# Moving every large SBUF tile from byte offset 64 to offset 0 within 128

## The chip, the cores and the metric

The kernel runs on one core of a Trainium2 chip. The metric is device time in microseconds, the median of several executions. A profile of one execution, with every instruction and every DMA packet, stands beside the times.

## The reference

One block of a streaming encoder, float32, 512 tokens of width 1024:

```python
proj = x @ w_in[layer]
q_a, k_a, v_a, q_i, k_i, w_i, q_s, k_s, v_s, g_a, g_b = jnp.split(proj, IN_OFFSETS, axis=-1)
w_i = w_i * IDX_HEADS ** -0.5
y_a = ...   # sparse attention, 8 heads of 64: an indexer (q_i, k_i, w_i) picks the 128 best keys of each query,
            # logits + relative bias, softmax, times v_a
y_s = ...   # stick-breaking attention, 8 heads of 64: exp(log_sigmoid(z) + sum of later log_sigmoid(-z)), times v_s
gate_a = jax.nn.sigmoid(g_a + b_gates[layer, 0])
gate_b = jax.nn.sigmoid(g_b + b_gates[layer, 1])
merged = gate_a * (y_a @ w_branch_dsa[layer]) + gate_b * (y_s @ w_branch_sb[layer])
x = layer_norm(DEEPNORM_ALPHA * x + merged @ w_out[layer], ln1_g[layer], ln1_b[layer])
u, g = jnp.split(x @ w_ffn_in[layer], 2, axis=-1)          # 2 x 2816 columns
h = jax.nn.gelu(causal_dwconv(u, conv_w[layer], conv_b[layer])) * g
x = layer_norm(DEEPNORM_ALPHA * x + h @ w_ffn_out[layer], ln2_g[layer], ln2_b[layer])
```

## The kernel before

**Precision.** Each operand of a product is split into a high part (rounded to the float32r type) and a low part (the rest), and each product is three matmuls: high x high, high x low, low x high. In the names, `h`/`hi` and `l`/`lo` are the two parts: `x1h` and `x1l` are the normed activations, `whi_u` and `wlo_u` a weight tile. Almost every matmul has a moving operand of 512 float32 columns (2 KB in a partition), with 384 in the first projection and 256 in some products.

**Weights.** The class `Stream` walks one list of pieces, mostly 128 x 1024 float32. For each, SP's queue loads a `raw` tile (L87), ACT makes the high part (L105), DVE or POOL the low part (L107). `raw` and the two rings have three buffers each, and loads and splits run three pieces ahead of use.

**Stages.** Indexer's projection `qi` (L249 to L251) and its keys `ki`; then attention heads, eight of each kind, with the remaining projections (`proj_t`, L285 to L287, and `proj_v`) and gates cut into groups of three matmuls and filled in between the heads' steps; transposes of the attention weights against `ident` (L420); branch projections, the output projection (L697 to L699) with the first norm; the FFN's two input products (`ffn_in`, L739 to L741), of which `u` goes through a causal convolution of width 3 (`activate`, L749 to L754), and the output product (`product`, L829 to L831), in which seven products of halves stand for eight; then the second norm. The order of the instructions on each engine is fixed when the program is built.

**Addresses.** SBUF is filled from both edges. Pools of tiles without a side are stacked upward from the left edge: first `cst` with the constants `ident` (512 bytes in each partition), `mhalf` (4), `bgt` (64), `cwt` (352) and `wi`, then the raw tiles, the rings and the stages' tiles. Pools with `side="right"` are stacked downward from the right edge; the first of them, `edge`, holds `rb` alone. An allocation begins at a multiple of 32 bytes, and large tiles take multiples of 128 bytes. Small ones are brought up to that by a helper:

```python
n = int(np.prod(shape[1:]))
t = pool.tile([shape[0], -(-n // 32) * 32], dt, **kw)[:, :n]
```

So all tiles of one side have the same offset within 128 bytes, and the first small tiles on that side set it. In the built program the tiles behind `cwt` and those behind `rb` all begin at 64 within 128 bytes; `ident`, against which transposes are made, begins at 0, `bgt` at 32 and `cwt` at 96.

`bgt` holds the gates' biases: 16 columns, read one at a time as ACT's bias (L546 and others). `rb` holds the relative bias table's high and low parts: 64 x 8, the weights of two matmuls (L270).

Of the kernel before, what the change touches and what calls it, by code (L numbers as in the profile page):

```python
# [11 lines left out]
F32 = mybir.dt.float32  # L12
F32R = mybir.dt.float32r
# [7 lines left out]
H = 8  # L21
# [109 lines left out]
def tile_block(ctx: ExitStack, tc: tile.TileContext, xT, xN, w_qi, w_ki, w_t, w_v, w_br, w_o, w_fi, w_fo,  # L131
# [10 lines left out]
    def padded(pool, shape, dt=F32, **kw):  # L142

        n = int(np.prod(shape[1:]))
        t = pool.tile([shape[0], -(-n // 32) * 32], dt, **kw)[:, :n]
        return t if len(shape) == 2 else t.rearrange("p (a b) -> p a b", a=shape[1])

    cst = ctx.enter_context(tc.tile_pool(name="cst", bufs=1))
    edge = ctx.enter_context(tc.tile_pool(name="edge", bufs=1, side="right"))
# [68 lines left out]
    nc.gpsimd.memset(mhalf, -0.5)  # L218
    nc.scalar.activation(mhalf, mhalf, AF.Sigmoid)
    nc.gpsimd.memset(mhalf, -0.5)  # L220
    bgt = cst.tile([128, 16], F32, name="bgt")
    cwt = cst.tile([128, FC, 4], F32, name="cwt")


# [31 lines left out]

    ohf = bp.tile([64, NREL], F32, tag="beta", bufs=2, name="ohf")
    oh = bp.tile([64, NREL], F32R, tag="beta", bufs=2, name="oh")
    rb = edge.tile([64, H], F32R, name="rb")
    rbf = padded(bp, [32, H], name="rbf")  # L260
    for r in (slice(0, 32), slice(32, 64)):
        nc.gpsimd.dma_start(ohf[r], onehot)
# [791 lines left out]
```

## Time and profile before

| | us |
|---|---|
| median of 3 executions | 762.42 |
| lowest, highest | 762.22, 762.43 |
| profiled execution | 762.05 |
| its span, first to last instruction | 760.2 |
| TensorE busy | 751.1 |
| VectorE, ScalarE, GpSimd busy | 547.1, 374.1, 119.3 |

The mean granted clock of TensorE over the span is 0.998 of full speed. PE stands for TensorE's matmuls, PEld for its weight loads, which run beside them, DVE for VectorE, ACT for ScalarE, POOL for GpSimd, SP for SyncE. A matmul's recorded duration includes its way through the array, so it is longer than the distance from its start to the next one's.

### The profile page before, as it was taken

The numbers are of one execution on the slowest core, as the hardware profiler recorded it, in microseconds if no ns is written. First come the engines' busy times: TensorE is split into PE (matmuls) and PEld (weight loads), VectorE is DVE, ScalarE is ACT, GpSimd is POOL, SyncE is SP. The second block draws the span as 40 slices with busy tenths as digits, with TensorE's granted clock in tenths as the row PEclk, the third lists the DMA queues.
The fourth block names the chain that finished last, engine by engine and source line by source line (L and its number), as shares of the span: only waits on it lengthen the run. The fifth ranks groups of instructions, "written<-read, shape, count | busy, mean of one in ns | idle before, by whom it ended". The sixth has DMA issues, their size and how long they took to land.

```text
span 760.2 us, 9908 instructions
## 1 busy us (share of the span) xinstructions
PE 751.1 (99%) x3597; PEld 630.3 (83%) x3597; DVE 547.1 (72%) x912; ACT 374.1 (49%) x601; POOL 119.3 (16%) x127
## 2 busy tenths in 40 slices
PE   9999999999999999999999999999999999999996
PEld 7788888888888888888889888888888888888885
DVE  6689587999675454458865778767877786777776
ACT  6554656555686857935311534433443443344320
POOL 3002555425834210000010000000000000000011
PEclk9999999999999999999999999999999999999999
DMA  8643423132333333126801554354434434445971
GB/s 258 225 155 100 123 83 111 57 111 84 111 98 97 102 106 99 55 78 203 328 1 42 166 181 147 117 180 170 135 138 164 169 129 147 168 153 157 340 291 56
DMA packets 38449, 107.09 MB, mean 141 GB/s; under 512 B 4536, under 2 KB 4936, under 8 KB 38400
## 3 DMA queue, kind: packets, MB, share of 16 engines
q1 hardware_dynamic: 34016, 95.73, 37.1%
q10 hardware_dynamic: 2576, 6.29, 3.2%
q0 software_dynamic: 1808, 4.44, 1.8%
q8 instruction: 28, 0.46, 0.2%
q14 instruction: 21, 0.17, 0.1%
HBM read 91.48 MB, written 12.87 MB: 137 GB/s over the span
## 4 chain that ended last, share of the span: by engine, by line
PE 92%; POOL 3%; issue 2%; DVE 2%; ACT 1%; DVEq 0%; POOLq 0%
PE u_ps L741 5%; PE u_ps L740 5%; PE g_ps L741 5%; PE u_ps L739 5%; PE g_ps L740 5%; PE g_ps L739 5%; PE m_ps L829 4%; PE m_ps L831 4%; PE m_ps L830 4%; PE av_ps L436 2%; PE ga_ps L285 2%; PE ga_ps L286 2%; PE ga_ps L287 2%; PE o_ps L698 2%; PE o_ps L699 2%
## 5 line engine op out<-in xcount | busy, mean ns | idle before, releaser
L739 PE MATMUL u_ps<-x1h,whi_u 128*128 128x512 f32 (+1 forms) x192 | 71.4, 372 | 0.0
L741 PE MATMUL u_ps<-x1h,wlo_u 128*128 128x512 f32 (+1 forms) x192 | 71.4, 372 | 0.0
L740 PE MATMUL u_ps<-x1l,whi_u 128*128 128x512 f32 (+1 forms) x192 | 71.3, 371 | 0.0
L739 PE MATMUL g_ps<-x1h,whi_g 128*128 128x512 f32 (+1 forms) x184 | 69.9, 380 | 0.0
L740 PE MATMUL g_ps<-x1l,whi_g 128*128 128x512 f32 (+1 forms) x184 | 69.9, 380 | 0.0
L741 PE MATMUL g_ps<-x1h,wlo_g 128*128 128x512 f32 (+1 forms) x184 | 69.9, 380 | 0.0
L748 POOL MEMSET u<- 128x2 f32 x22 | 2.1, 100 | 250.1 <-DVE c L753 250.1
L740 PEld LDWEIGHTS u_ps<-x1l,whi_u 128*128 128x128 f32 x192 | 36.2, 188 | 6.3
L739 PEld LDWEIGHTS u_ps<-x1h,whi_u 128*128 128x128 f32 x192 | 36.2, 188 | 6.2
L741 PEld LDWEIGHTS u_ps<-x1h,wlo_u 128*128 128x128 f32 x192 | 36.2, 188 | 6.2
L740 PEld LDWEIGHTS g_ps<-x1l,whi_g 128*128 128x128 f32 x184 | 34.6, 188 | 6.6
L739 PEld LDWEIGHTS g_ps<-x1h,whi_g 128*128 128x128 f32 x184 | 34.6, 188 | 6.5
L741 PEld LDWEIGHTS g_ps<-x1h,wlo_g 128*128 128x128 f32 x184 | 34.6, 188 | 6.5
L425 DVE TENSOR_TENSOR ptl<-tr_ps,pth 128x512 fp32r<-128x512 f32 (+1 forms) x48 | 27.4, 595 | 14.0 <-ACT pth L424 13.7
L107 DVE TENSOR_TENSOR wlo_u<-raw,whi_u 128x1024 fp32r<-128x1024 f32 x22 | 26.9, 1221 | 9.8 <-ACT whi_u L105 9.8
L105 ACT ACTIVATE whi_g<-raw 128x1024 fp32r<-128x1024 f32 x22 | 23.3, 1061 | 20.5 <-PE m_ps L831 13.6
L105 ACT ACTIVATE whi_pa<-raw 128x1024 fp32r<-128x1024 f32 x11 | 11.7, 1061 | 40.8 <-PE u_ps L740 32.3
L754 ACT ACTIVATE c<-c,cwt 128x512 f32<-128x512 f32 x22 | 15.8, 716 | 30.0 <-DVE c L753 30.0
L105 ACT ACTIVATE whi_u<-raw 128x1024 fp32r<-128x1024 f32 x22 | 23.3, 1060 | 13.9 <-PE u_ps L740 9.0
L107 DVE TENSOR_TENSOR wlo_g<-raw,whi_g 128x1024 fp32r<-128x1024 f32 x22 | 26.8, 1218 | 3.1 <-ACT whi_g L105 3.1
L488 POOL TENSOR_TENSOR bm<-win,score 128x256 f32<-128x256 f32 (+2 forms) x24 | 26.9, 1148 | 9.0 <-DVE mn L503 8.9
L758 DVE TENSOR_TENSOR hp<-g_ps,c 128x512 f32<-128x512 f32 x22 | 15.2, 691 | 17.3 <-PE g_ps L741 15.8
(559 smaller groups left out, 2205.9 us busy)
## 6 DMA issues: line engine op xcount, KB each, us to landing
raw<-in_w_fi_dram SPq DMA_DIRECT2D x44, 512.0 KB, 3.3
raw<-in_w_t_dram SPq DMA_DIRECT2D x32, 512.0 KB, 3.3
raw<-in_w_fo_dram SPq DMA_DIRECT2D x21, 512.0 KB, 3.5
rawb_p<-in_w_fo_dram SPq DMA_DIRECT2D x11, 512.0 KB, 3.7
d_z<-s_sum SPq DMA_DIRECT2D x10, 512.0 KB, 7.4
raw<-in_w_v_dram SPq DMA_DIRECT2D x8, 512.0 KB, 4.3
raw<-in_w_br_dram SPq DMA_DIRECT2D x8, 512.0 KB, 3.3
raw<-in_w_o_dram SPq DMA_DIRECT2D x8, 512.0 KB, 4.3
```

Source lines behind the costliest of these rows:

```text
L105: nc.scalar.activation(hi[:, :w], t[:, :w], AF.Copy)
L107: self.low = eng.tensor_sub(lo[:, :w], t[:, :w], r32(hi[:, :w])).ins
L285: nc.tensor.matmul(ps[:M], wh[:, c], xh[k], start=(k == 0), stop=False)
L425: lows = nc.vector.tensor_sub(tl[:, :width], ps[:, :width], r32(th[:, :width]))
L488: nc.gpsimd.tensor_add(bm[:, OFF[j]:OFF[j] + N], win[:, 512 - N:512], score[j])
L739: nc.tensor.matmul(ps[:, c], wh[:, kc], x1h[:, k, c], start=(k == 0), stop=False)
L740: nc.tensor.matmul(ps[:, c], wh[:, kc], x1l[:, k, c], start=False, stop=False)
L741: nc.tensor.matmul(ps[:, c], wl[:, kc], x1h[:, k, c], start=False, stop=(k == KC - 1))
L754: nc.scalar.activation(c, c, AF.Gelu_apprx_tanh, bias=cwt[:, f, 3:4])
L829: nc.tensor.matmul(o, xh_[:, r], wh[:, c], start=start, stop=False, skip_group_check=True)
L830: nc.tensor.matmul(o, xh_[:, r], wl[:, c], start=False, stop=False, skip_group_check=True)
L831: mm = nc.tensor.matmul(o, xl_[:, r], wh[:, c], start=False, stop=stop, skip_group_check=True)
```

## The change

Two small tiles are made 64 bytes longer, and the same slice of them as before is used: `bgt` at the left edge, from 64 to 128 bytes, and `rb` at the right edge, from 32 to 96 bytes. All that is stacked behind them moves by 64 bytes: upward on the left, downward on the right. In the built program these tiles then begin at 0 within 128 bytes; `cwt` begins at 32. No instruction is added, removed or moved.

```diff
@@ -218,7 +218,7 @@
     nc.gpsimd.memset(mhalf, -0.5)
     nc.scalar.activation(mhalf, mhalf, AF.Sigmoid)
     nc.gpsimd.memset(mhalf, -0.5)
-    bgt = cst.tile([128, 16], F32, name="bgt")
+    bgt = cst.tile([128, 32], F32, name="bgt")[:, :16]
     cwt = cst.tile([128, FC, 4], F32, name="cwt")
@@ -256,7 +256,7 @@
     ohf = bp.tile([64, NREL], F32, tag="beta", bufs=2, name="ohf")
     oh = bp.tile([64, NREL], F32R, tag="beta", bufs=2, name="oh")
-    rb = edge.tile([64, H], F32R, name="rb")
+    rb = edge.tile([64, 24], F32R, name="rb")[:, :H]
     rbf = padded(bp, [32, H], name="rbf")
```

## The prediction

> **What bounds the kernel now.** I read the page first, for who is busy and what the chain of waits consists of.
>
> ```profile
> span 760.2 us, 9908 instructions
> PE 751.1 (99%) x3597; PEld 630.3 (83%) x3597; DVE 547.1 (72%) x912; ACT 374.1 (49%) x601; POOL 119.3 (16%) x127
> ...
> PE 92%; POOL 3%; issue 2%; DVE 2%; ACT 1%; DVEq 0%; POOLq 0%
> ```
>
> TensorE is busy nearly from end to end and is 92% of the chain that ends last. Second, the table by stage, since a share over the whole span could hide a stage with another limit (columns: length, then busy time of PE, PEld, DVE, ACT, POOL, then clock, DMA share, GB/s).
>
> ```profile
> 0.00:21.00 21.00, 19.80 (x96) 16.75 (x97) 12.22 (x20) 12.70 (x21) 6.04 (x19) 1.00 0.86 264
> ...
> 50.00:160.00 110.00, 110.00 (x539) 92.81 (x538) 93.02 (x186) 64.40 (x116) 46.71 (x27) 1.00 0.31 94
> 160.00:208.00 48.00, 47.68 (x241) 40.02 (x240) 40.18 (x78) 27.95 (x55) 28.55 (x20) 1.00 0.34 104
> 208.00:330.00 122.00, 122.00 (x608) 102.83 (x607) 65.31 (x130) 91.12 (x167) 23.55 (x23) 1.00 0.29 92
> ...
> 414.00:690.00 276.00, 276.00 (x1261) 230.29 (x1259) 206.64 (x299) 119.05 (x165) 3.13 (x22) 1.00 0.45 152
> 690.00:744.00 54.00, 54.00 (x242) 44.78 (x241) 38.34 (x55) 16.86 (x19) 1.98 (x2) 1.00 0.76 267
> 744.00:760.30 16.30, 8.65 (x68) 8.25 (x66) 12.44 (x24) 0.51 (x1) 2.78 (x3) 0.91 0.18 65
> ```
>
> From 21 to 744 us PE never rests for long; only the last 16 us belong to DVE (12.44 us against PE's 8.65). Third, PE's own waits. There are two in the whole span:
>
> ```profile
> PE idle_ps L208 <- DVE idle L205: 1.2, 1, 1.2
> PE gb_ps L285 <- DVE va L337: 0.3, 1, 0.3
> ```
>
> So a DMA, ACT or DVE instruction that gets a few ns longer or shorter has almost nowhere to show. What counts is the time from one matmul's start to the next. Fourth, then, the timeline of PE, once for each width of moving operand: 512 columns in the FFN, 384 in the first projection (four merged in a row), 256 in the last product.
>
> ```profile
> 559.82 0.39 PE L740 MATMUL u_ps<-x1l,whi_u 128*128 128x512 f32 x1
> ...
> 561.86 0.39 PE L740 MATMUL u_ps<-x1l,whi_u 128*128 128x512 f32 x1
> ...
> 7.75 0.85 PE L249 MATMUL qi_ps<-xh,whi_qi 128*128 128x384 f32 x4
> 8.44 0.85 PE L250 MATMUL qi_ps<-xl,whi_qi 128*128 128x384 f32 x4
> ...
> 747.81 0.28 PE L829 MATMUL m_ps<-d_z,eh 128*128 128x256 f32 x1
> 747.93 0.28 PE L830 MATMUL m_ps<-d_z,eh 128*128 128x256 f32 x1
> ```
>
> Between the first two rows stand nine matmuls' starts: 2.04 / 9 = 227 ns for 512 columns. Then 0.69 / 4 = 173 ns for 384 and 120 ns for 256. From 256 to 512 columns the step is 107 ns, so 512 columns alone would take 2 x 107 = 214 ns, and each matmul carries about 13 ns that does not depend on its width (384: 173 - 160 = 13). This fixed 13 ns is the only thing in the profile through which a start address could move the time much. In the layout of the built program every moving operand of these matmuls starts at 64 within 128 bytes, so the trace has no row of the same matmul at 0.
>
> **The change part by part.** It adds, removes and reorders no instruction; on every engine the rows are the same. In the layout, 930 buffers counted from the left edge move up by 64 bytes and 97 counted from the right edge down by 64; all these stood at 64 and then stand at 0. cwt goes from 96 to 32; ident, mhalf and bgt stay. The extra columns of bgt and rb are never written or read: their DMA and their two DVE instructions have the same size, so 0 us.
>
> Weight loads. 3597, beside the matmuls (188 ns of 227). Here the trace has start offsets to compare: the eight slices of wlo_ki follow each other by 72 x 4 = 288 bytes, so they start at 64, 96, 0 and 32 within 128, twice over.
>
> ```profile
> L287 PEld LDWEIGHTS ki_ps<-xh,wlo_ki x8: 140/141/142, 23.2 to 28.1; 128*72 128x72 f32 x8
> ```
>
> Minimum to maximum 2 ns: the start offset is not seen. Cost 0; the cover is 227 - 188 = 39 ns a matmul, and losing it would need a load 39 ns longer.
>
> DVE and ACT. The convolution reads u at its start (64), and 4 and 8 bytes later, and ACT writes u 8 bytes later; the same shapes at 64 stand beside them.
>
> ```profile
> L752 DVE SCALAR_TENSOR_TENSOR c<-u,cwt,c x22: 743/745/754, 423.9 to 685.4; 128x512 f32<-128x512 f32 x22
> L753 DVE SCALAR_TENSOR_TENSOR c<-u,cwt,c x22: 742/748/753, 425.2 to 686.2; 128x512 f32<-128x512 f32 x22
> ...
> L670 DVE SCALAR_TENSOR_TENSOR r<-r,rstd,ln x14: 741/743/746, 376.8 to 752.2; 128x512 f32<-128x512 f32 x14
> ...
> L749 ACT ACTIVATE u<-u_ps x22: 579/580/585, 421.1 to 683.7; 128x512 f32<-128x512 f32 x22
> ...
> L424 ACT ACTIVATE pth<-tr_ps 128x512 fp32r<-128x512 f32 x32 | 18.2, 588 | 4.9 <-PE tr_ps L420 4.8
> ```
>
> Shifts of 4 and 8 bytes cost DVE 2 to 5 ns of 743 and ACT nothing (580 against 588). Taken as the bound of a shift by 64 bytes: 5 / 743 = 0.7% either way on the part of the chain that is not PE (POOL 3%, DVE 2%, ACT 1%: 6% of 760.2 = 46 us), +-0.3 us. I take 0; POOL has no row of its own and goes by DVE's.
>
> DMA. The same transfers, with other addresses in SBUF. PE's two waits end on DVE, none on a DMA, and the 21 us in which the DMA share is 0.86 have PE busy for 19.8. What hides them is that loads run three pieces ahead. If that cover went, the exposed part is the first 4.79 us, before which no real matmul starts; a change of 5% there would be +-0.2 us. I take 0.
>
> Matmuls. 3597, less 192 transposes (rows below) and 9 warm-up ones: 3396, of which 92% on the chain: 3124. A price of the new offset cannot be read, so bounds. Below: the whole fixed 13.3 ns goes, 3124 x 13.3 = 41.5 us gained. Above: the spacing that matmuls have elsewhere in this trace, where it is longest. Groups by form, durations of the same 128x512 matmul:
>
> ```profile
> L739 PE MATMUL g_ps<-x1h,whi_g 128*128 128x512 f32 x168 | 65.4, 389 | 0.0
> ...
> L285 PE MATMUL qa_ps<-xh,whi_qa 128*128 128x512 f32 x32 | 12.8, 399 | 0.0
> ...
> L285 PE MATMUL qs_ps<-xh,whi_qs 128*128 128x512 f32 x32 | 12.5, 390 | 0.0
> ...
> L420 PE MATMUL tr_ps<-ident,lg 128*128 128x128 f32 x80 | 12.0, 272 | 0.0
> ...
> L420 PE MATMUL tr_ps<-ident,beta 128*128 128x128 f32 x80 | 10.7, 272 | 0.0
> ...
> L720 PE MATMUL xt_ps<-ident,r 128*128 128x128 f32 x32 | 4.3, 272 | 0.0
> ```
>
> That is 399 - 389 = 10 ns more; 3124 x 10 = 31 us lost at most. Between ends so far apart I take 0, by two rows. The weight loads, the one PE operation seen at both offsets, do not differ. And qs, qa and g_ps have their operands at the same 64 and still differ by 1 to 10 ns, so a good part of what a matmul carries beyond its columns comes from what runs around it and not from its address.
>
> Sum: 0 + 0 + 0 + 0 against the profiled execution's 762.05 us (span 760.2 and 1.8 around it). The median of the runs is 762.42, 0.4 above; I forecast 762.4. Without another timing to go by I take 0.2% (1.5 us) as about what a measurement can tell from no change.
>
> **The rivals.** First, a large gain: PE fetches the moving operand in blocks of 128 bytes, and an operand that starts in the middle of one needs 17 blocks instead of 16. 128 bytes are 32 columns, 32 x 107 / 256 = 13.4 ns, which is just the fixed part found above, for each of the three widths. Then the change removes it: 762.4 - 41.5 = 721 us. DVE would allow that (206.6 of 276 us in the longest stage). For it speaks the size; against it, that a fixed start of a matmul would look the same, and that the fixed part is not constant at a constant offset.
>
> The Trainium skill speaks for this rival too: "TensorE: Matmul & The Clock Gate", section "Part 1: The HAM clock gate (the "warmup" mystery)", gives warm back-to-back matmuls as N / 2.4 GHz plus about 2.5 ns, 215.7 ns for 512 columns. This trace has 227. If the missing 11 ns were the offset's, an estimate by that page is 3124 x 10.8 = 34 us, 729 us; the page's figure was not taken on fp32 operands, and no row here has it.
>
> Second, slower: at 0 the moving operand and the weights both begin on the edge of such a block, and their reads, which run at the same time, meet, as something does between 21 and 330 us, where the qa matmuls take 10 ns more. Its place is the stage from 414 to 744 us, now free of it. Price: 1261 + 242 = 1503 matmuls x 10 ns = 15 us, 777 us if all are hit; it decides (beyond 1.5 us) once 150 are, one in ten. Against it: the weight loads' indifference to their own offset.
>
> Third, a small gain: left and right tiles move in opposite directions, and the longer spacing of 21 to 330 us, whatever causes it, goes down. There some 1400 matmuls (539 + 241 + 608 in the rows above) have a mean excess between 1 and 10 ns; with 4 ns, the whole of it is 5.6 us, and half is 759.6 us.
>
> **How the numbers follow.** No measurable change 0.70 (761 to 763.9). Large gain 0.08 (721). Small gain 0.08 (757 to 760.8). Slower 0.14: it starts just over 764 and reaches 777, about half below 768. So faster 0.16, same 0.70, slower 0.14. The range 758.5 to 768 takes in the first case, most of the small gain and half of the slower one: 0.70 + 0.06 + 0.07 = 0.83.
>
> **What would show it.** Right: the 512-column rows of the FFN again 0.227 us apart, the 256-column ones 0.12, weight loads 188, DVE 743 to 748, PE's two waits the same. The first rival shows as 0.213 to 0.216 us in the FFN and 107 to 109 ns for 256 columns, with PE waiting for DVE in the attention stages. The second shows as 389 turning to some 399 ns in L739 to L741. The third shows in the L285 to L287 groups alone. I am wrong if the fixed 13 ns is the offset's, which only the timing of a matmul at 0 can tell.

## The result and the profile after

The changed kernel takes 773.14 us (median of 4 executions, 772.40 to 773.62) where the kernel before takes 762.42: ratio 1.0134, interval 1.0120 to 1.0148. The change costs 10.7 us; I had forecast none. The page, profiled execution of the changed kernel (772.76 us):

```profile
span 771.0 us, 9908 instructions
...
PE 761.8 (99%) x3597; PEld 630.0 (82%) x3597; DVE 547.3 (71%) x912; ACT 374.5 (49%) x601; POOL 119.3 (15%) x127
```

PE's busy time grew by 10.7 us, that of the weight loads and of the other engines by 0.4 us at most. PE still waits for nothing to speak of:

```profile
PE idle_ps L208 <- DVE idle L205: 1.2, 1, 1.2
PE qi_ps L249 <- ACT whi_qi L105: 0.3, 1, 0.3
```

So the same 3597 matmuls stand further apart in time. The timeline of PE in the FFN:

```profile
540.05 0.39 PE L739 MATMUL u_ps<-x1h,whi_u 128*128 128x512 f32 x1
...
544.72 0.39 PE L741 MATMUL u_ps<-x1h,wlo_u 128*128 128x512 f32 x1
```

20 distances lie between these rows: 4.67 / 20 = 233.5 ns, against 227 before. But not every matmul changed. The groups by form (mean duration in ns at the second place behind the bar), first after, then two rows of before that the prediction did not show:

```profile
L739 PE MATMUL g_ps<-x1h,whi_g 128*128 128x512 f32 x168 | 66.3, 395 | 0.0
...
L829 PE MATMUL m_ps<-whi_pa,gh 128*128 128x512 f32 x44 | 17.1, 389 | 0.0
...
L285 PE MATMUL qs_ps<-xh,whi_qs 128*128 128x512 f32 x32 | 12.6, 395 | 0.0
...
L829 PE MATMUL m_ps<-d_z,eh 128*128 128x512 f32 x11 | 4.3, 395 | 0.0
```

```profile
L829 PE MATMUL m_ps<-whi_pa,gh 128*128 128x512 f32 x44 | 17.1, 389 | 0.0
...
L829 PE MATMUL m_ps<-d_z,eh 128*128 128x512 f32 x11 | 4.3, 389 | 0.0
```

The FFN's input product went from 389 to 395 ns, qs from 390 to 395. Of the output product, the group `whi_pa,gh` stayed at 389, though both its operands moved from 64 to 0 as well; the group `d_z,eh`, on the same line, went from 389 to 395. Summing the distances from start to start over the 512-column matmuls by line, L739 to L741 went from 223.0 to 229.4 us (+6.4), L285 to L287 from 183.3 to 186.1 (+2.8), L829 to L831 from 97.2 to 98.0 (+0.8).

What tells the groups apart is the side of SBUF. In L739 and L285 the moving operand (x1h, xh) lies on the right and the weights on the left, and so it is for `d_z` and `eh`; for `whi_pa` and `gh`, as for 120 of the 143 matmuls of 512 columns on L829, both lie on the left. The change moves the left up by 64 and the right down by 64, so across the two sides the distance changes by 128. I sorted the distances of consecutive 512-column matmuls by (start of the moving operand less start of the weights that are loaded beside it, those of the next matmul) within 256 bytes:

| trace, 414 to 692 us | difference 0 | difference 128 |
|---|---|---|
| before | 226.7 ns (1182) | none |
| after | 228.0 ns (180) | 233.2 ns (958) |

The kernel before has such pairs too, between 20 and 340 us: 72 at a difference of 128 take 232.2 ns on average, 920 at 0 take 228.5 (counted where the matmul before the pair has 512 columns too). From here on theory A is: what counts is this difference within 256 bytes, and 0 is good. Its rivals: B, a start at 0 within 128 is bad in itself; C, a moving operand at 128 within 256 is bad, wherever the weights are.

### The profile page after: what moved, and what is told of

Its sections match the earlier page's. It is cut to its first block, busy times and chain, and to the rows that moved or that the text cites. A ratio compares the mean times of both kernels' runs of the same rounds, so it can differ in the third digit from the quotient of the medians.

```text
span 771.0 us, 9908 instructions
## 1 busy us (share of the span) xinstructions
PE 761.8 (99%) x3597; PEld 630.0 (82%) x3597; DVE 547.3 (71%) x912; ACT 374.5 (49%) x601; POOL 119.3 (15%) x127
## 4 chain that ended last, share of the span: by engine, by line
PE 96%; DVE 1%; DMA 1%; SPq 0%; ACT 0%; issue 0%; DVEq 0%; ACTq 0%
PE u_ps L741 5%; PE u_ps L739 5%; PE u_ps L740 5%; PE g_ps L741 5%; PE g_ps L740 5%; PE g_ps L739 5%; PE m_ps L829 4%; PE m_ps L830 4%; PE m_ps L831 4%; PE av_ps L436 3%; PE tr_ps L420 2%; PE gb_ps L287 2%; PE ga_ps L285 2%; PE ga_ps L286 2%; PE ga_ps L287 2%; PE gb_ps L286 2%
## 5 line engine op out<-in xcount | busy, mean ns | idle before, releaser
L739 PE MATMUL u_ps<-x1h,whi_u 128*128 128x512 f32 (+1 forms) x192 | 72.3, 377 | 0.0
L741 PE MATMUL u_ps<-x1h,wlo_u 128*128 128x512 f32 (+1 forms) x192 | 72.3, 376 | 0.0
L741 PE MATMUL g_ps<-x1h,wlo_g 128*128 128x512 f32 (+1 forms) x184 | 70.8, 385 | 0.0
L739 PE MATMUL g_ps<-x1h,whi_g 128*128 128x512 f32 (+1 forms) x184 | 70.8, 385 | 0.0
L739 PEld LDWEIGHTS u_ps<-x1h,whi_u 128*128 128x128 f32 x192 | 36.1, 188 | 7.3
L741 PEld LDWEIGHTS u_ps<-x1h,wlo_u 128*128 128x128 f32 x192 | 36.1, 188 | 7.3
L739 PEld LDWEIGHTS g_ps<-x1h,whi_g 128*128 128x128 f32 x184 | 34.5, 188 | 7.6
L741 PEld LDWEIGHTS g_ps<-x1h,wlo_g 128*128 128x128 f32 x184 | 34.5, 188 | 7.5
```

Source lines behind the costliest of these rows:

```text
L739: nc.tensor.matmul(ps[:, c], wh[:, kc], x1h[:, k, c], start=(k == 0), stop=False)
L741: nc.tensor.matmul(ps[:, c], wl[:, kc], x1h[:, k, c], start=False, stop=(k == KC - 1))
```

## The experiments

**All tiles at 0, sides alike within 256.** Like the change, but the right side goes down by 192 and not by 64.

```diff
-    bgt = cst.tile([128, 16], F32, name="bgt")
+    bgt = cst.tile([128, 32], F32, name="bgt")[:, :16]
-    rb = edge.tile([64, H], F32R, name="rb")
+    rb = edge.tile([64, 56], F32R, name="rb")[:, :H]
```

> Every large tile at 0 within 128 bytes, as in the changed kernel, but the right edge is moved down by 192 bytes and not by 64, so that moving operand and next weights again start alike within 256 bytes (3134 of the matmuls, as in the kernel before; 796 in the changed one). Theory A (what counts is the distance of the moving operand's start from the start of the weights that are loaded meanwhile, within 256 bytes: 0 is good, 128 bad): 762.4 us, FFN matmuls 227 ns apart. Theory B (offset 0 within 128 is bad in itself): 773 us, 232 to 233 ns apart. Theory C (a moving operand at 128 within 256 is bad, wherever the weights are; here it is at 0): 762.4 us.

Measured: 762.64 us, ratio to before 1.0000 (0.9990 to 1.0011). Its group by form:

```profile
L739 PE MATMUL g_ps<-x1h,whi_g 128*128 128x512 f32 x168 | 65.4, 389 | 0.0
```

All tiles are at 0 and nothing is lost: B falls.

**All tiles stay at 64, the left side moved by 128.**

```diff
-    bgt = cst.tile([128, 16], F32, name="bgt")
+    bgt = cst.tile([128, 48], F32, name="bgt")[:, :16]
```

> Every large tile stays at 64 within 128 bytes, as in the kernel before; only the left edge's tiles move, up by 128. The moving operands on the right stay at 192 within 256, the weights on the left go from 192 to 64, so they differ by 128. Theory A: 773 us, FFN matmuls 232 to 233 ns apart, like the changed kernel's. Theory B: 762.4 us, since no offset within 128 changes. Theory C: 762.4 us, since the moving operands do not change.

Measured: 773.36 us, ratio 1.0137 (1.0118 to 1.0156), the whole loss with no tile at another offset within 128, and with the right side's moving operands where they were: C falls too. The group by form is that of the changed kernel:

```profile
L739 PE MATMUL g_ps<-x1h,whi_g 128*128 128x512 f32 x168 | 66.3, 395 | 0.0
```

**Each half of the change alone.** First bgt's line of the diff only (`[128, 32]`).

> One half of the change: bgt alone is longer, rb is as before. Left tiles at 0 within 256, right ones stay at 192: the distance is 192 within 256. Theory A: slower than before; by how much is not known, since the trace has only three such pairs (233.7 ns before, 232.3 after the change); with 233 ns, 773 us. Theory B: somewhere between, since only the left tiles stand at 0: about 768 us. Theory C: 762.4 us.

Measured: 772.37 us, ratio 1.0123 (1.0108 to 1.0138). Then rb's line only (`[64, 24]`).

> The other half of the change: rb alone is longer, the right tiles go from 192 to 128 within 256, the left ones stay at 192. The difference is 192 (as with the left edge alone, which took 772.4 us). Theory A: 772.4 us too, so that each half alone costs what both together cost. If the cost came from what lies at 0 or 128 on one side, it would differ from that of the other half, and the two would add up to the whole 10.7 us: about 763 us.

Measured: 772.88 us, ratio 1.0136 (1.0121 to 1.0151). Each half costs nearly what both cost together; they do not add up. Either half alone leaves a difference of 192 across the sides, at which the FFN's pairs take 233.3 ns; both together leave 128, at which they take 233.2. That is the mark of a relation between two addresses: once it is broken, breaking it further costs little.

**The spacing by itself.** Series of 48 matmuls on PE alone, nothing beside them, with other start offsets in each series; one execution. An entry of `CASES` is kind (f float32r, b bfloat16), columns, and the bytes at which moving operand and weights begin.

```python
CASES = [("f", 512, 0, w) for w in (0, 32, 64, 96, 128, 160, 192, 224, 256)]
CASES += [("f", 512, m, w) for m, w in ((64, 64), (64, 192), (128, 128), (128, 0), (192, 192), (192, 64))]
...
for n in range(COUNT):
    mo = m + (n % 4) * 512
    wo = w + (n % 8) * 256
    nc.tensor.matmul(acc[c % 8][:, :N], b[:, wo:wo + 128], a[:, mo:mo + N],
                     start=(n == 0), stop=(n == COUNT - 1), skip_group_check=True)
```

> Not the reference's computation: PE alone does 25 series of 48 matmuls with nothing beside them, each series with other start offsets of moving operand and weights; the output is a sum of them. Theory A: the spacing depends on the difference alone: 512 columns 226.7 ns where the two starts are equal within 256 (0 and 0, 0 and 256, 64 and 64, 128 and 128, 192 and 192, 16 and 16), some 232 ns at a difference of 128, whatever the offsets themselves; between, values for 32, 64, 96, 160, 192, 224 that are not known. Theory B: 64 and 64, 64 and 192, 192 and 64 at 227, and 0 and 0, 0 and 128, 128 and 0 at 232. Theory C: only 128 and 128, 128 and 0 slow. bfloat16, half the bytes: no difference expected by any.

The timeline of its PE; a series begins where its row begins, so the difference of two neighbouring starts is 48 distances. The rows: moving 0 and weights 128; 160 (for its start alone); 192; 224 (start alone); 256; then 64 and 64; 64 and 192; 128 and 128 (start alone).

```profile
59.67 11.32 PE L43 MATMUL acce<-mov,wts 128*128 128x512 f32 x48
70.83 11.37 PE L43 MATMUL accf<-mov,wts 128*128 128x512 f32 x48
82.03 11.16 PE L43 MATMUL accg<-mov,wts 128*128 128x512 f32 x48
93.03 11.36 PE L43 MATMUL acch<-mov,wts 128*128 128x512 f32 x48
104.22 11.04 PE L43 MATMUL acca<-mov,wts 128*128 128x512 f32 x48
115.10 11.09 PE L43 MATMUL accb<-mov,wts 128*128 128x512 f32 x48
126.03 11.32 PE L43 MATMUL accc<-mov,wts 128*128 128x512 f32 x48
137.19 11.09 PE L43 MATMUL accd<-mov,wts 128*128 128x512 f32 x48
...
243.32 10.31 PE L43 MATMUL accg<-movb,wtsb 128*128 128x512 bf16 x47
253.47 10.52 PE L43 MATMUL acch<-movb,wtsb 128*128 128x512 bf16 x47
```

0 and 128: 11.16 / 48 = 232.5 ns. 0 and 192: 11.00 / 48 = 229.2. 0 and 256: 10.88 / 48 = 226.7, as at 0 and 0. 64 and 64: 10.93 / 48 = 227.7, of which the first ten are unsettled (224 to 236 ns) and the rest 226.7. 64 and 192: 232.5. Means without the first 16 of a series, from the same start times:

| moving, weights (bytes within 256) | ns |
|---|---|
| 0, 0; 64, 64; 128, 128; 192, 192 | 226.7 |
| 0, 192 (moving 64 past the weights) | 228.9 |
| 0, 128; 64, 192; 128, 0; 192, 64 | 232.2 to 232.6 |
| 0 with 32, 64, 96, 160, 224 | 233.3 to 234.4 |
| 0 with 4, 16 | 232.5, 233.3 |
| 16, 16 | 233.3 |

The loss at a difference of 128 is there with nothing else running, so neither DMA nor another engine is part of it: this much of theory A holds. Two things were not as expected: a difference of 64 is nearly as good as 0, and at 16 and 16 equal starts do not help. With 384 columns the loss at a difference of 128 is smaller (176.0 against 173.3 ns), with 256 it turns round (118.5 against 120.0), and in bfloat16 there is none (216 ns in both).

**The same with other offsets and narrower weights.** One execution again. The second entry of a case is now the number of weight columns; "s" takes the same weights each time, "a" moves every second weight by 128 bytes.

```diff
+CASES = [("f", 128, m, w) for m, w in ((0, 0), (64, 0), (128, 64), (192, 128), (0, 64), (0, 192))]
+CASES += [("f", 128, m, m) for m in (8, 32, 48, 96)]
+CASES += [("f", 128, 0, w) for w in (128 + 256, 192 + 256, 208, 176)]
+CASES += [("f", M, 0, w) for M in (96, 64, 32) for w in (0, 128)]
+CASES += [("s", 128, 0, 0), ("s", 128, 0, 128), ("a", 128, 0, 0), ("a", 128, 64, 0)]
```

> Not the reference's computation: again series of 48 matmuls of 512 columns with nothing beside them, with other offsets and with fewer weight columns. Expected from the series before: 0 and 0 226.7 ns; moving 64 past the weights (64 and 0, 128 and 64, 192 and 128, 0 and 192) 228.9 whatever the offsets; weights 64 past the moving (0 and 64) 233.4. 0 and 384 as 0 and 128 (232.4), 0 and 448 as 0 and 192 (228.9), if 256 is the period. For equal starts that are no multiple of 64 bytes (8, 32, 48, 96) not known; 16 and 16 took 233.3, so if multiples of 64 are needed, all four take 233. Weight columns 96, 64, 32 at 0 and 0: if the 13.3 ns beyond 512 columns come from the weight load's reads, they shrink in proportion to 10, 6.7 and 3.3 ns (223, 220, 217); if they are a fixed start of each matmul, 226.7. At 0 and 128 the excess over that shrinks too in the first case. Weights that alternate between two places: if the next weights' place counts, every second spacing is long.

Its timeline: 64 and 0; 128 and 64 (start alone); then 0 and 192; 8 and 8; 32 and 32; 48 and 48 (start alone); then weights of 32 columns at 0 and 0, the same at 0 and 128, and the next series' start.

```profile
26.60 11.17 PE L41 MATMUL accb<-mov,wts 128*128 128x512 f32 x48
37.61 11.16 PE L41 MATMUL accc<-mov,wts 128*128 128x512 f32 x48
...
70.80 11.36 PE L41 MATMUL accf<-mov,wts 128*128 128x512 f32 x48
82.00 11.35 PE L41 MATMUL accg<-mov,wts 128*128 128x512 f32 x48
93.19 11.07 PE L41 MATMUL acch<-mov,wts 128*128 128x512 f32 x48
104.09 11.20 PE L41 MATMUL acca<-mov,wts 128*128 128x512 f32 x48
...
214.59 11.27 PE L41 MATMUL accc<-mov,wts 128*32 128x512 f32 x48
225.69 11.24 PE L41 MATMUL accd<-mov,wts 128*32 128x512 f32 x48
236.77 11.07 PE L41 MATMUL acce<-mov,wts 128*128 128x512 f32 x48
```

64 and 0: 11.01 / 48 = 229.4 ns (settled 228.8, like 128 and 64, 192 and 128); 0 and 64: settled 233.4, so the sign counts. 0 and 384, 0 and 448 come out as 0 and 128, 0 and 192 did in the first program (232.6, 228.9), so 256 is the period.

One series does not fit theory A: 0 and 192 itself, 228.9 in the first program, takes 11.20 / 48 = 233.3 ns here. It stands behind the series at 0 and 64 and goes on with the same distances, 233 and 234 ns. So the two addresses do not settle the spacing alone; what ran before can count too, and a value measured once, as at 16 and 16 (also 233 and 234), may be such a leftover. With weights of 128 columns, equal starts at multiples of 32 settled at 226.7 each time, whatever stood before them, and a difference of 128 never did.

Equal starts at other places: 8 and 8 take 233.1; 32 and 32 227.1 (settled 226.7, as at 96 and 96); 48 and 48 settle at 230.0. So equal starts are good at the multiples of 32 that were tried and not at 8, 16, 48. Narrower weights do not shorten the distance: 32 columns take 11.10 / 48 = 231.3 ns. The 13 ns beyond 512 columns' own time thus do not shrink with the weight load. Nor does a difference of 128 cost the narrowest anything: 32 columns take 11.08 / 48 = 230.8 ns there, 64 columns 229.3 against 230.2 at equal starts; 96 columns lose 1.7 ns. The loss of 6 ns is shown for weights of 128 columns only. The same weights each time ("s") give 226.7 and 232.2 ns, as different ones do. That every second weight lies elsewhere ("a") gives 232.1 and 231.2 ns with a pattern of six distances, from which it can't be told whether the next or the present weights' place counts.

**A difference of 64 in the kernel.** bgt at 256 bytes, the left side moved by 192.

```diff
-    bgt = cst.tile([128, 16], F32, name="bgt")
+    bgt = cst.tile([128, 64], F32, name="bgt")[:, :16]
```

> The kernel before with bgt at 256 bytes, so that the left tiles move by 192: the weights go from 192 to 128 within 256, the moving operands on the right stay at 192, and the difference (moving less weights) is 64 in 2308 matmuls. Alone, a series at this difference took 228.9 ns, where 0 took 226.7 and all others 232 or more. Theory A with the values of that series: 2308 x 2.2 ns = 5 us, about 767 us, clearly between the kernel before and the changed one. If only equal starts are good: 773 us.

Measured: 766.41 us, ratio 1.0047 (1.0032 to 1.0062), against 767 from the series. Its timeline in the FFN:

```profile
559.93 0.39 PE L739 MATMUL g_ps<-x1h,whi_g 128*128 128x512 f32 x1
...
561.08 0.39 PE L740 MATMUL g_ps<-x1l,whi_g 128*128 128x512 f32 x1
```

Five rows are one after another up to the second: 1.15 / 5 = 230 ns; the mean over the 983 pairs at this difference from 414 to 692 us is 229.1.

**All at 32, sides alike.**

```diff
-    bgt = cst.tile([128, 16], F32, name="bgt")
+    bgt = cst.tile([128, 40], F32, name="bgt")[:, :16]
-    rb = edge.tile([64, H], F32R, name="rb")
+    rb = edge.tile([64, 48], F32R, name="rb")[:, :H]
```

> Left tiles up by 96, right ones down by 160: every large tile at 32 within 128 bytes, and moving operands and weights again alike within 256 (32 and 32), in the same 3134 matmuls as before. Theory A: 762.4 us, 226.7 ns in the FFN, since series at 32 and 32 and at 96 and 96 took 226.7. If multiples of 64 are wanted for anything in this kernel: slower, some 233 ns and 773 us if it is PE.

Measured: 763.29 us, ratio 1.0012 (1.0002 to 1.0021), and the FFN's matmuls are back:

```profile
L739 PE MATMUL g_ps<-x1h,whi_g 128*128 128x512 f32 x168 | 65.4, 389 | 0.0
```

Alikeness within 256 gives back all but some 0.8 us; what those are, if they are more than scatter, stays open.

**More pairs alike.** rbf at 256 bytes, which puts the attention's tiles on the same offset within 256 as the rest.

```diff
-    rbf = padded(bp, [32, H], name="rbf")
+    rbf = bp.tile([32, 64], F32, name="rbf")[:, :H]
```

> The kernel before with one small tile longer in another place: rbf takes 256 bytes and not 128, so that the attention's tiles behind it move from 64 to 192 within 256. Then moving operand and next weights start alike within 256 in 3371 matmuls and not in 3134; all stay at 64 within 128. Theory A: faster. The 72 pairs of 512 columns that differ by 128 between 20 and 340 us get some 5 ns each back, 0.4 us, and the 920 alike ones there, which take 228.5 ns on average because each odd pair throws the next ten out of step, at most 1.8 ns each, 1.7 us: 0.4 to 2.1 us, 760.3 to 762.0 us. Theory B and C: 762.4 us, as no offset within 128 changes and the projections' moving operands stay where they are.

Measured: 762.21 us against 762.90 of the kernel before on the same chip, ratio 0.9994 (0.9985 to 1.0002): a gain is not shown, and the time lies outside the 760.3 to 762.0 that were expected. In the trace the 512-column pairs between 20 and 340 us take 228.1 ns and not 228.5.

Then, in addition, `bgt` allocated ahead of `ident`:

```diff
+    bgt = cst.tile([128, 16], F32, name="bgt")
     ident = cst.tile([128, 128], F32, name="ident")
...
-    bgt = cst.tile([128, 16], F32, name="bgt")
     cwt = cst.tile([128, FC, 4], F32, name="cwt")
```

> As the one before it, and bgt is allocated ahead of ident, so that ident, the moving operand of the transposes, starts at 192 within 256 like the weights beside it. Theory A, if a transpose throws the next matmuls out of step only through this difference: the remaining part of the 1.7 us, 0.5 to 1 us less than the one before it. If a transpose does that in any case (its spacing is 107 ns and not that of a 512-column matmul): the same as the one before it.

Measured: 761.96 us, ratio 0.9990 (0.9980 to 0.9999); 228.0 ns. This is the fastest version, by 0.1%; from the one before it, it can't be told apart, as expected if a transpose disturbs in any case. What goes with these pairs' staying above 226.7 in the traces: after each odd matmul (a transpose, 128 columns) the spacing wanders between 224 and 236 ns for about ten matmuls before it settles, as at the beginning of the series above.

## Why the prediction was wrong

**The bound was right.** PE set the end before and after; DVE, ACT and DMA had no share in the loss. L752 and L753 (743/748/754 and 743/750/753 after, against 743/745/754 and 742/748/753) and L749 (580 both) show it in the changed kernel. Those zeros of the sum stand.

**The step that failed** is "Matmuls", where I took 0 "by two rows" and the runs show 10.7 us, 10.0 of them in the three groups of lines above. The first, that weight loads last the same at 64, 96, 0 and 32, answers another question: a load takes 188 ns in the changed kernel too, but the matmul beside it gets its next start later. The matmuls that ran beside those loads stand one row further in the same answer:

```profile
L287 PE MATMUL ki_ps<-xh,wlo_ki x8: 391/392/397, 23.5 to 28.3; 128*72 128x512 f32 x8
```

392 and not 389 ns, though their 72-column weights would have kept that from being proof. The second, that qs, qa and g_ps differ by 1 to 10 ns "at the same 64", was a mean read as if every matmul had it. First before, then with rbf at 256 bytes (minimum, median, maximum in ns):

```profile
L285 PE MATMUL qa_ps<-xh,whi_qa x32: 387/389/478, 141.0 to 278.5; 128*128 128x512 f32 x32
```

```profile
L285 PE MATMUL qa_ps<-xh,whi_qa x32: 389/389/482, 141.4 to 278.9; 128*128 128x512 f32 x32
```

The median of qa is the FFN's 389; three of its 32 matmuls, directly behind a transpose or another matmul of 128 columns, take 446 to 478 ns and make most of the mean's 399. They stay long where the pairs there are alike. So those 10 ns do come from what runs around, as I had said; but that something else moves the duration does not show that the address cannot.

**The step before it**: I described the layout by the offset within 128, as the change's own words do, and so took all tiles of before for alike. Within 256 they happened to be alike across the two sides too (192 and 192), and the change, which moves the sides in opposite directions, ended that (128 on the right, 0 on the left). I had written that last fact down, under the third rival, as a possible gain.

**The first rival** (blocks of 128 bytes, 721 us) is out: the fixed 13 ns are the same at 0 and 0 as at 64 and 64, 226.7 ns. The Trainium skill's figure behind it holds for bfloat16: those series run 10.15 us for 47 recorded matmuls, 216 ns, which agrees with the 215.7 in "TensorE: Matmul & The Clock Gate", section "Part 1: The HAM clock gate (the "warmup" mystery)"; float32r takes 226.7 here. What the further 11 ns are stays open.

**The second rival** (reads of moving operand and weights meet, 777 us if all 1503 matmuls are hit) named the right pair of operands, with a chance of 0.14, but the wrong condition: equal starts are the good case, not the bad one. That its time came near the measured one is luck: the 10 ns were qa's mean. The price is 233.2 - 226.7 = 6.5 ns by the pairs of 414 to 692 us; the 984 matmuls of 512 columns in L739 to L741 make 6.4 us of it, and L285 to L287 add 2.8, which I had left out of that price.

**The third rival** (a small gain in L285 to L287, 759.6 us) had the place but the wrong sign: these lines lost 2.8 us.

## What to carry to other kernels

A change of an address is a change of its distance from every other operand: sort the spacing of the bound engine's instructions by the offsets of all operands and their differences, at several powers of two, before taking an alignment for harmless. In this kernel float32r matmuls of 512 columns with 128 weight columns want moving operand and weights to begin alike within 256 bytes; one small tile at an edge decides over 1.3% of the time. The duration of an instruction beside the bound one does not price it either: the weight loads stayed at 188 ns. And before a difference of means is taken for a price, look at the median.

## What was not expected of the hardware

The spacing of float32r matmuls depends on how the addresses of moving operand and weights stand to each other. With 512 moving and 128 weight columns and no other engine at work it is 226.7 ns at equal starts within 256 bytes (multiples of 32), 228.9 where the moving operand begins 64 past the weights (233.3 in one series of six), and 230 to 234 at the other differences tried, as at equal starts of 8, 16 and 48 bytes. The Trainium skill says in "TensorE: Matmul & The Clock Gate", section "Part 2: What happens when you issue a matmul", that PE has two independent read ports to SBUF and that loading the next weights takes no read bandwidth from the running matmul. The series disagree in so far as the place of the weights alone changes the spacing of the matmuls by 6 ns; whether that is a shared bank, a shared queue or something else they do not tell. And the good spacing is a state that has to be reached: after a disturbance it takes about ten matmuls at equal starts (224 to 236 ns, then 226 and 227).
